# First folded weights of u made ahead of retention's last norm, constants moved off the vector engine, and other groups in the order of fours

## The chip, the cores and the metric

The kernel runs on one core of one Trainium2 chip. The metric is the time of one execution on the device, in microseconds (us); lower is better. A core has a matrix engine (TensorE, PE in the profile, its weight loads PEld), a vector engine (VectorE, DVE), a scalar engine (ScalarE, ACT), a general engine (GpSimd, POOL) and a queue engine (SyncE, SP) that issues the loads. Each engine works through its own instructions in order; semaphores join them.

## The reference

Two layers over 256 tokens of width 2048, with a second stream of 256 context tokens, batch 1, all in float32. Cut to what matters:

```python
# layer 0 (even): one input projection, two paths, one output projection
qx, kx, vx, gax, ux, gbx = _split_even(hx @ w_in)      # the same for the context: k and v
ret_x = _retention(rope(qx), rope(kx), vx, ...)        # 8 heads, both directions,
                                                       # each head's output divided by its rms
y_a = merge(ret_x) * silu(gax)
y_b = einsum(real(fft2(ux over tokens and channels of a group)), fno_w) * silu(gbx)
x   = x + gate * (concat(y_a, y_b) @ w_out)
# layer 1 (odd)
bg, cg, xt, g = split(h @ w_in1, 4)                    # 4 x 4096 columns
x   = x + gate * ((bg * conv3(cg * xt) * silu(g)) @ w_out1)
return rmsnorm(x)
```

Before each layer there is a modulated rmsnorm whose shift, scale and gate come from a conditioning vector times `ada_w`.

## The kernel before, in words

**Products in two halves.** Every weight and activation is cut into a high part in the rounded format float32r and a low part, the rest. A product is high times high, high times low and low times high. `cut` makes a high part with a copy on ACT (line 94) and the rest with a subtraction on DVE (line 59). Cut weights live in `slot()`s: rings of six `whi` and six `wlo` tiles of 128 x 512.

**Loads.** `load_raw` (line 85) fetches a weight tile of 128 x 2048 (1 MB) on SP's queue into a ring of three `raw` buffers. `split_w` cuts it in four pieces.

**Groups.** `group_t` computes 256 columns of a projection, transposed, for all tokens: `nkt` tiles of weights, four pieces each, and in each piece four blocks j of 128 x 128 with two matmuls: H (the high weights against both parts of the activations, 512 columns) and L (the low weights against the high part, 256 columns). The order of the eight is one of three lists: LOW (L0 H0 L1 H1 ...), HIGH (H0 L0 H1 L1 ...) and FOURS (H0 H1 H2 H3 L0 L1 L2 L3). The argument `orders` gives the list for the first piece and for all others. `lr` adds the two halves of a result on ACT (line 198) and DVE (line 65).

**Order of the work.** After every second piece `group_t` calls `hook()`, which takes the next function of the list `stages`: other work of the layer is laid in between so. `bg()` takes a task from a list of 64 reductions over `adaT`. The compiler's scheduler then orders the instructions of each engine by its own model of readiness; the written order is its priority.

**Stages of layer 0.** First the modulation, then four pairs of heads (`pr` 0 to 3): keys, queries and values, two groups for the gate (`sga`), with a head's `scores`, `values` and `norm` as stages. `norm` of a head is a matmul with ones into `ss`, a root on ACT (line 206), a reciprocal on DVE (line 207) and a product; the last norm of the last head is `h1[2]()` after the two gate groups of pair 3. Then `split_act` makes `yA`. Here the tile pool `rp` of retention closes, and the pool `fp` of the Fourier path opens on the same memory: its first writes wait for the last uses of `rp`.

**Fourier path.** The transform over tokens is folded: `fold_x` makes sums and differences of token pairs in `hf` (DVE lines 65, 68 and `split_act`); the first four of its eight tiles are made during pair 3, the others inside the `steps`. The weights of u are folded too: `half.fold(kc)` loads `w0u` (one load for two kc), makes the sum and the difference of two 512-column blocks with `add` (line 65) and `dif` (line 68) into tiles `ef` of the pool `fp`, and cuts both. `half.step(kc)` multiplies: six matmuls into `pu` and two into `pd`, 16 steps in each of two halves `u0` and `u1`; at its end it makes the next fold. The `pd` matmuls hold the end tokens (token 0 and 128 of the fold): their left side is `sd`, a tile of 16 x 32 columns, zero but for two columns that `ends(e)` copies out of `hf[e]`. `e0`, `rest`, `zero`, `umf` and `zero4` are constants that DVE fills (lines 590 to 612).

Between the steps runs `gate_of(g)` for g 0 to 7, a `group_t` of two tiles of `w0g` each. The stages from `gate_of(0)` on are:

```python
stages += [None, None, None, steps(0), steps(1), steps(2), steps(3, 4), ...]
```

so that step 0 comes at the fourth hook, behind the last piece of `gate_of(0)`.

**Projections.** `project` computes the output of a layer in eight blocks of 256 columns: seven `group_t` of four tiles (128 matmuls) and a last block `group_d`. Block 1 has orders (HIGH, FOURS), block 2 (HIGH, LOW), all others LOW. It runs once for each layer. The odd layer has 16 blocks b of four `group_t` of two tiles (64 matmuls): `tcg`, `txt`, `tbg`, `tg`. In b 1 and 2 `tcg` has (HIGH, FOURS) and `txt` (HIGH, LOW); all others are LOW.

Of the kernel before, what the change touches and what calls it, by code (L numbers as in the profile page):

```python
# [24 lines left out]
P = 128  # L25
# [10 lines left out]
def body(tc, a, out):  # L36
    nc = tc.nc
    es = ExitStack()
    with es:
# [43 lines left out]
        def load_raw(src):  # L83
            raw = wp.tile([P, 2048], F32, tag="raw", name="raw")
            nc.sync.dma_start(raw[:], src)
            return raw

        def slot():
            return (wp.tile([P, 512], F32R, tag="whi", bufs=6, name="whi")[:],
                    wp.tile([P, 512], F32R, tag="wlo", bufs=6, name="wlo")[:])  # L90
# [37 lines left out]
        HIGH = "H0 L0 H1 L1 H2 L2 H3 L3".split()  # L128
        FOURS = "H0 H1 H2 H3 L0 L1 L2 L3".split()

        SETTLE, AFTER = (HIGH, FOURS), (HIGH, LOW)

        def group_t(wd, i0, nkt, streams, orders=(LOW, LOW)):

            ps = [psum("gT") for _ in streams]
            last = nkt * 8 - 1
            for kt in range(nkt):
                raw = load_raw(wd[i0 + kt])
                bg()
                for pc, (hi, lo) in enumerate(split_w(raw)):  # L140
                    todo = orders[kt + pc > 0]
                    seen = set()
                    for what, j in ((x[0], int(x[1])) for x in todo):
                        k2, m = j // 2, j % 2
                        kc, c0 = kt * 8 + pc * 2 + k2, j * 128
                        n = 512 if what == "H" else 256
                        w = (hi if what == "H" else lo)[:, c0:c0 + 128]
                        for t, st in zip(ps, streams):
                            mm(t[:, m, 0:n], w, st[kc // 2][:, kc % 2, 0:n], kc == 0 and j not in seen,
                               kc == last and j in seen)  # L150
                        seen.add(j)
                    if pc % 2:
                        hook()
            return ps
# [331 lines left out]
        for pr in range(4):  # L486
            mk = [masks(2 * pr), masks(2 * pr + 1)]
            vbox = []
            def keys():
                tk, tkc = group_t(w0, iw[0], 2, [hx, hc])  # L490
                iw[0] += 2
                return rope(lr(rp, tk)[:], "k", K_CK, K_SK), lr(rp, tkc, "kc", 1)

            def queries():
                tq, = group_t(w0, iw[0], 2, [hx])
                iw[0] += 2
                return rope(lr(rp, tq)[:], "q", K_CQ, K_SQ)
# [12 lines left out]
            def heads():  # L510
                return [retention(hh, mk[hh], q, k, kc, lambda: vbox[0]) for hh in range(2)]

            if pr == 0:
                kc = rp.tile([P, 2, 256], F32, tag="kc", bufs=1, name="kc")
                nc.scalar.copy(kc[:], pk[:, 1, :].rearrange("p (m t) -> p m t", m=2))
                k = rope(pk[:, 0, :].rearrange("p (m t) -> p m t", m=2), "k", K_CK, K_SK)
                q = rope(pq[:].rearrange("p (m t) -> p m t", m=2), "q", K_CQ, K_SQ)
                h0, h1 = heads()
                stages += [None, h0[0], h1[0], h0[1], h0[2], h1[1], None, h1[2]]
                keep((pvx, pvc))  # L520
            elif pr < 3:
                k, kc = keys()
                q = queries()
                h0, h1 = heads()
                stages += [None, h0[0], None, h1[0], None, None, None, None]
                stages += [None, h0[1], None, h0[2], None, h1[1], None, h1[2]]
                keep(values())
            else:
                k, kc = keys()
                stages += [None, lambda: fold_x(rp, 0), None, None, None, lambda: fold_x(rp, 1), None, None]  # L530
                keep(values())
                stages += [None, lambda: fold_x(rp, 2), None, lambda: fold_x(rp, 3)]
                quiet[0] = True
                q = queries()
                h0, h1 = heads()
                stages += [h0[0], None, h0[1], h1[0], h0[2], None, h1[1], None]
            sga = []
            for hh in range(2):
                tg, = group_t(w0, iw[0], 2, [hx])
                iw[0] += 2  # L540
                sga.append(silu_lr(rp, tg, "sga"))
            if pr == 3:
                h1[2]()
            for hh, hd in enumerate((h0, h1)):
                y = yA[2 * pr + hh] = act_tile(YA[2 * pr + hh], f"yA{2 * pr + hh}")
                t = hd[3]["t"]
                mul(t[:], t[:], sga[hh][:])
                split_act(y, t[:])
# [38 lines left out]
            tab.update(dm=dm, dmh=dmh, dml=dml)  # L587

        e0 = fp.tile([P, 32], F32, name="e0")
        nc.vector.memset(e0[:], 0.0)  # L590
        nc.vector.memset(e0[:, 0:1], 1.0)
        rest = fp.tile([P, 1], F32, name="rest")
        nc.vector.memset(rest[:], 1.0)
        nc.vector.memset(rest[0:1, :], 0.0)
        sd = fp.tile([P, 16, 32], F32R, name="sd")
        zero = fp.tile([P, 512], F32, tag="t2", bufs=4, name="zero")
        nc.vector.memset(zero[:], 0.0)
        nc.vector.tensor_copy(sd[:], zero[:].rearrange("p (k c) -> p k c", k=16))

        def ends(e):  # L600
            nc.vector.tensor_copy(sd[:, 2 * e:2 * e + 2, 0:1], hf[e][:, :, 128:129].bitcast(F32))
            nc.vector.tensor_copy(sd[:, 2 * e:2 * e + 2, 1:2], hf[e][:, :, 384:385].bitcast(F32))

        for e in range(4):
            ends(e)
        umf = fp.tile([P, 16], F32, name="umf")
        nc.vector.memset(umf[:], 0.0)
        umh = fp.tile([P, 16], F32R, name="umh")
        uml = fp.tile([P, 16], F32R, name="uml")

        zero4 = fp.tile([P, 4], F32, name="zero4")
        nc.vector.memset(zero4[:], 0.0)

        ys = yA + [None] * 8

# [26 lines left out]
        class half:  # L642


            def __init__(self, hf):
                self.hf, self.pu = hf, None

            def fold(self, kc):

                if kc % 2 == 0:  # L650
                    self.raw = load_raw(a["w0u"][self.hf * 8 + kc // 2])
                r = self.raw[:].rearrange("p (k s c) -> p k s c", k=2, s=2)[:, kc % 2, :, :]
                self.w = []
                for op in (add, dif):
                    x = fp.tile([P, 512], F32, tag="ef", bufs=2, name="ef")
                    op(x[:], r[:, 0, :], r[:, 1, :])
                    self.w.append(slot())
                    cut(x[:], *self.w[-1])

            def step(self, kc):  # L660
                if self.pu is None:
                    self.pu, self.pd = psum("pu"), bank("pd")
                    self.fold(0)
                k2, w = kc % 2, self.w
                x = hf[kc // 2]
                for s in range(2):
# [122 lines left out]
        def steps(*kcs):  # L789
            def f():  # L790
                for kc in kcs:
                    u0.step(kc)
                    folds(kc)()
            return f

        stages += [None, None, None, steps(0), steps(1), steps(2), steps(3, 4), steps(5), steps(6), steps(7, 8), steps(9),
                   steps(10), steps(11, 12), both(steps(13), setup_tables), both(steps(14), setup_middle), both(steps(15), gs[0][0])]
        for g in range(4):
            gate_of(g)
# [27 lines left out]
        def project(wd, xs, gcol, xin, acc, first=None, post=None):  # L827
# [7 lines left out]
            for b in range(8):  # L835
                src = xin(b)
                quiet[0] = b >= 7 - (post is not None)
                if b < 7:
                    t = first if b == 0 and first is not None else group_t(wd, 4 * b, 4, [xs], *({1: (SETTLE,), 2: (AFTER,)}.get(b, ())))[0]
# [43 lines left out]
        w1 = a["w1"]  # L883
        y1 = []
        for b in range(16):
            tcg, = group_t(w1, b * 8, 2, [h1], *((SETTLE,) if b in (1, 2) else ()))
            scg = lr(l1, tcg, "scg", 2)
            txt, = group_t(w1, b * 8 + 2, 2, [h1], *((AFTER,) if b in (1, 2) else ()))
            z = lr(l1, txt, "z", 2)
            mul(z[:], z[:], scg[:])  # L890
            cv = l1.tile([P, 2, 256], F32, tag="cv", bufs=2, name="cv")
            for m in range(2):
# [5 lines left out]
                                               op0=ALU.mult, op1=ALU.add)  # L898
                nc.vector.scalar_tensor_tensor(c4[:, :, 0:63], z4[:, :, 1:64], w[2], c4[:, :, 0:63],
                                               op0=ALU.mult, op1=ALU.add)  # L900
            tbg, = group_t(w1, b * 8 + 4, 2, [h1])
            sbg = lr(l1, tbg)
            mul(cv[:], cv[:], sbg[:])
            tg, = group_t(w1, b * 8 + 6, 2, [h1])
            sg = silu_lr(l1, tg, "t2", 5)
            mul(cv[:], cv[:], sg[:])
            y1.append(act_tile(YA[b] if b < 8 else f"hx{b - 8}", f"y1_{b}"))
# [125 lines left out]
```

## Time and profile before

| | |
|---|---|
| median of three runs | 1823.37 us |
| lowest and highest of them | 1822.88 and 1826.58 us |
| the profiled execution, its own time | 1826.86 us |
| its span, mean granted clock | 1825.1 us, 0.988 |
| matmuls | 10086 |
| loads | 399.16 MB on SP's queue |

The span is the time from the first to the last instruction of the profiled execution; its own time has the start and the end beside it. In the rows below, an instruction is named by engine, line of the kernel, operation and tiles (output<-inputs); "L59 DVE ... wlo<-raw,whi" is the subtraction of a cut. "x" is a count. The time after the bar is the busy time in us and the mean of one in ns; what follows a second bar, or stands in square brackets, is idle time ahead of it and what ended it. The chain of work that ended last is followed back from the last instruction, at each step to what released it. The granted clock is the share of full speed at which PE ran.

### The profile page before, as it was taken

Reading aid. Unit: us, or ns where it says so; the run is one execution under the profiler, and the core shown is the slowest. Engines: PE = TensorE matmul, PEld = TensorE weight load, DVE = VectorE, ACT = ScalarE, POOL = GpSimd, SP = SyncE. Lnnn points to the kernel's source line nnn. Section 1 sums busy time; section 2 is a strip of 40 time slices with the busy share of each in tenths; the row PEclk is TensorE's granted clock in tenths of the full one; section 3 lists DMA queues with packets and bytes.
Section 4 is the critical chain, followed back from the end, with each engine's and each line's share of the span. In section 5 each row is a group of like instructions: output and inputs, shape, how many; then the busy total and the mean of one; then the engine's idle time right before and its main releaser. Section 6 shows DMA issues by size and latency. Waiting matters only on the chain.

```text
span 1825.1 us, 25950 instructions
## 1 busy us (share of the span) xinstructions
PE 1777.8 (97%) x10086; PEld 1514.6 (83%) x10086; DVE 1248.0 (68%) x2001; ACT 901.9 (49%) x1493; POOL 0.2 (0%) x4
## 2 busy tenths in 40 slices
PE   5999999999989999999999999999999999999997
PEld 3667888888877888888978888888888888888887
DVE  5348858758469788777677888666666666665554
ACT  4225626345455455444555555555555555555553
POOL 0000000000000000000000000000000000000000
PEclk9999999999989899999999999999999999999999
DMA  9886656655435556577647777555555555555552
GB/s 388 341 315 259 233 212 221 240 207 208 166 117 217 199 188 216 194 295 295 231 155 264 296 277 281 197 191 185 187 196 195 185 185 191 197 189 185 187 193 105
DMA packets 58732, 400.82 MB, mean 220 GB/s; under 512 B 6512, under 2 KB 6896, under 8 KB 11376
## 3 DMA queue, kind: packets, MB, share of 16 engines
q1 hardware_dynamic: 58608, 399.16, 59.8%
q8 instruction: 79, 1.29, 0.3%
q14 instruction: 45, 0.37, 0.1%
HBM read 397.03 MB, written 2.10 MB: 219 GB/s over the span
## 4 chain that ended last, share of the span: by engine, by line
PE 94%; DVE 3%; DMA 1%; ACT 1%; issue 0%; SPq 0%; DVEq 0%; ACTq 0%
PE gT L56 71%; PE gN L56 7%; PE gD L56 3%; PE pu L56 2%; PE gemv L56 2%; PE o L56 2%; PE pk L56 1%; PE pvx L56 1%; PE pvc L56 1%; PE pd L56 1%; DMA raw<-ada 1%; PE S L56 1%; PE pq L56 1%; DVE wlo L59 1%; PE pP L56 1%; PE py L56 0%
## 5 line engine op out<-in xcount | busy, mean ns | idle before, releaser
L94 ACT CAST whi<-raw 128x512 fp32r<-128x512 f32 x1024 | 628.3, 620 | 627.3 <-PE gT L56 469.4
L59 DVE TENSOR_TENSOR wlo<-raw,whi 128x512 fp32r<-128x512 f32 x1024 | 693.2, 688 | 344.4 <-ACT whi L94 334.5
L56 PE MATMUL gT<-h,whi 128*128 128x512 f32 x2048 | 707.6, 394 | 0.7 <-DVE h L215 0.7
L56 PE MATMUL gT<-h,wlo 128*128 128x256 f32 x2048 | 560.8, 278 | 3.4 <-ACT h L214 3.4
L56 PEld LDWEIGHTS gT<-h,whi 128*128 128x128 f32 x2048 | 383.3, 188 | 89.0 <-DVE h L215 1.2
L56 PEld LDWEIGHTS gT<-h,wlo 128*128 128x128 f32 x2048 | 383.4, 188 | 5.6 <-ACT h L214 3.8
L56 PE MATMUL gT<-hx,whi 128*128 128x512 f32 x576 | 209.4, 398 | 0.0
L388 DVE CUSTOM_DVE_ANT_0 raw<-raw,scb 128x2048 f32<-128x2048 f32 x64 | 146.5, 2290 | 54.0 <-DMA raw<-adaT 50.8
L56 PE MATMUL gT<-hx,wlo 128*128 128x256 f32 x576 | 165.2, 287 | 2.8 <-ACT v L507 1.6
L56 PE MATMUL gT<-y,whi 128*128 128x512 f32 x448 | 150.9, 394 | 0.0
L56 PEld LDWEIGHTS gT<-hx,whi 128*128 128x128 f32 x576 | 108.8, 189 | 21.3
L56 PEld LDWEIGHTS gT<-hx,wlo 128*128 128x128 f32 x576 | 109.5, 190 | 10.0 <-DVE wlo L59 2.7
L56 PE MATMUL gT<-y,wlo 128*128 128x256 f32 x448 | 116.9, 278 | 0.0
L56 PEld LDWEIGHTS gT<-y,whi 128*128 128x128 f32 x448 | 82.9, 188 | 18.2
L198 ACT COPY lr_r<-gT 128x512 f32<-128x512 f32 x103 | 60.5, 587 | 65.7 <-PE gT L56 65.4
L56 PEld LDWEIGHTS gT<-y,wlo 128*128 128x128 f32 x448 | 82.1, 188 | 1.4
L56 PE MATMUL gT<-yA,whi 128*128 128x512 f32 x224 | 77.5, 398 | 0.0
L56 PE MATMUL gT<-yB,whi 128*128 128x512 f32 x224 | 76.9, 398 | 0.0
L65 DVE TENSOR_TENSOR t<-gT,lr_r 128x512 f32<-128x512 f32 x68 | 46.9, 689 | 29.9 <-ACT lr_r L198 29.7
L56 PE MATMUL gT<-yA,wlo 128*128 128x256 f32 x224 | 59.9, 281 | 0.6 <-DVE wlo L59 0.6
L56 PE MATMUL gN<-whi,hx 128*128 128x512 f32 x192 | 59.7, 392 | 0.0
L56 PE MATMUL gN<-whi,hc 128*128 128x512 f32 x192 | 59.7, 391 | 0.0
(283 smaller groups left out, 2162.0 us busy)
## 6 DMA issues: line engine op xcount, KB each, us to landing
raw<-w SPq DMA_DIRECT2D x168, 1024.0 KB, 4.8
raw<-adaT SPq DMA_DIRECT2D x64, 1024.0 KB, 4.9
raw<-ada SPq DMA_DIRECT2D x32, 1024.0 KB, 7.1
raw<-w0o SPq DMA_DIRECT2D x32, 1024.0 KB, 4.8
raw<-w1o SPq DMA_DIRECT2D x32, 1024.0 KB, 4.8
raw<-w0g SPq DMA_DIRECT2D x16, 1024.0 KB, 4.8
raw<-w0u SPq DMA_DIRECT2D x16, 1024.0 KB, 4.9
raw<-w0s SPq DMA_DIRECT2D x8, 1024.0 KB, 5.6
```

Of the source, the lines that this page charges most:

```text
L56: nc.tensor.matmul(o, l, r, start=start, stop=stop, skip_group_check=True)
L59: nc.vector.tensor_tensor(o, x, hi.bitcast(F32), op=ALU.subtract)
L65: nc.vector.tensor_tensor(o, x, y, op=ALU.add)
L94: nc.scalar.copy(hi, x)
L198: nc.scalar.copy(r[:], t[:, :, 256:512])
L388: nc.vector.tensor_tensor_reduce(out=raw[:], in0=raw[:], in1=scb[:], scale=1.0, scalar=0.0, op0=ALU.mult, op1=ALU.add, accum_out=gv[:, j:j ...
```

## The change

1. **First folds.** In pair 3, ahead of `h1[2]()`, the first tile of `w0u` is loaded and its four folds (kc 0 and 1, `add` and `dif`) are made into two tiles `first_u`, which lie in the memory of `hc[6]` and `hc[7]`, free by then. `fold(0)` and `fold(1)` of `u0` then only cut. `u0.fold(0)` becomes a stage of its own, one hook ahead of step 0.
2. **Constants and end tokens.** The fills of `e0`, `rest`, `zero`, `umf` and `zero4` go from DVE to GpSimd. The copy of zeros into `sd` and the copies of the end tokens go to ACT, one copy for the two columns where there were two.
3. **Fours.** `orders` is a list that the pieces take in turn. SETTLE is HIGH and seven FOURS, AFTER is HIGH and seven LOW: eight pieces, a group of two tiles. In `project`, blocks 3 and 4 have SETTLE + AFTER, block 1 and 2 nothing. In the odd layer `tbg` of b 0 and 1 has SETTLE and `tg` of b 0 and 1 AFTER, beside `tcg` and `txt` of b 1 and 2 as before.

```diff
-        SETTLE, AFTER = (HIGH, FOURS), (HIGH, LOW)
+        SETTLE, AFTER = [HIGH] + [FOURS] * 7, [HIGH] + [LOW] * 7
-        def group_t(wd, i0, nkt, streams, orders=(LOW, LOW)):
+        def group_t(wd, i0, nkt, streams, orders=(LOW,)):
...
-                    todo = orders[kt + pc > 0]
+                    todo = orders[(kt * 4 + pc) % len(orders)]
...
             if pr == 3:
+                raw = load_raw(a["w0u"][0])[:].rearrange("p (k s c) -> p k s c", k=2, s=2)
+                first_u = [acts.tile([P, 2, 512], F32, tag=HF[6 + k2], name="first_u") for k2 in range(2)]
+                for k2 in range(2):
+                    for i, op in enumerate((add, dif)):
+                        op(first_u[k2][:, i, :], raw[:, k2, 0, :], raw[:, k2, 1, :])
                 h1[2]()
...
-        nc.vector.memset(e0[:], 0.0)
-        nc.vector.memset(e0[:, 0:1], 1.0)
+        nc.gpsimd.memset(e0[:], 0.0)
+        nc.gpsimd.memset(e0[:, 0:1], 1.0)
...
-        nc.vector.memset(zero[:], 0.0)
-        nc.vector.tensor_copy(sd[:], zero[:].rearrange("p (k c) -> p k c", k=16))
+        nc.gpsimd.memset(zero[:], 0.0)
+        nc.scalar.copy(sd[:], zero[:].rearrange("p (k c) -> p k c", k=16))
         def ends(e):
-            nc.vector.tensor_copy(sd[:, 2 * e:2 * e + 2, 0:1], hf[e][:, :, 128:129].bitcast(F32))
-            nc.vector.tensor_copy(sd[:, 2 * e:2 * e + 2, 1:2], hf[e][:, :, 384:385].bitcast(F32))
+            nc.scalar.copy(sd[:, 2 * e:2 * e + 2, 0:2], hf[e][:, :, 128:512:256].bitcast(F32))
...
             def fold(self, kc):
+                self.w = []
+                if self.hf == 0 and kc < 2:
+                    for i in range(2):
+                        self.w.append(slot())
+                        cut(first_u[kc][:, i, :], *self.w[-1])
+                    return
...
-        stages += [None, None, None, steps(0), ...
+        stages += [None, None, lambda: u0.fold(0), steps(0), ...
...
-                    t = ... group_t(wd, 4 * b, 4, [xs], *({1: (SETTLE,), 2: (AFTER,)}.get(b, ())))[0]
+                    t = ... group_t(wd, 4 * b, 4, [xs], SETTLE + AFTER if b in (3, 4) else (LOW,))[0]
...
-            tbg, = group_t(w1, b * 8 + 4, 2, [h1])
+            tbg, = group_t(w1, b * 8 + 4, 2, [h1], SETTLE if b in (0, 1) else (LOW,))
...
-            tg, = group_t(w1, b * 8 + 6, 2, [h1])
+            tg, = group_t(w1, b * 8 + 6, 2, [h1], AFTER if b in (0, 1) else (LOW,))
```

More of the change, by code (lines that the diff above doesn't have):

```diff
@@ L589, in body @@
         e0 = fp.tile([P, 32], F32, name="e0")
-        nc.vector.memset(e0[:], 0.0)
-        nc.vector.memset(e0[:, 0:1], 1.0)
+        nc.gpsimd.memset(e0[:], 0.0)
+        nc.gpsimd.memset(e0[:, 0:1], 1.0)
         rest = fp.tile([P, 1], F32, name="rest")
-        nc.vector.memset(rest[:], 1.0)
-        nc.vector.memset(rest[0:1, :], 0.0)
+        nc.gpsimd.memset(rest[:], 1.0)
+        nc.gpsimd.memset(rest[0:1, :], 0.0)
         sd = fp.tile([P, 16, 32], F32R, name="sd")
         zero = fp.tile([P, 512], F32, tag="t2", bufs=4, name="zero")
-        nc.vector.memset(zero[:], 0.0)
-        nc.vector.tensor_copy(sd[:], zero[:].rearrange("p (k c) -> p k c", k=16))
+        nc.gpsimd.memset(zero[:], 0.0)
+        nc.scalar.copy(sd[:], zero[:].rearrange("p (k c) -> p k c", k=16))
         def ends(e):
-            nc.vector.tensor_copy(sd[:, 2 * e:2 * e + 2, 0:1], hf[e][:, :, 128:129].bitcast(F32))
-            nc.vector.tensor_copy(sd[:, 2 * e:2 * e + 2, 1:2], hf[e][:, :, 384:385].bitcast(F32))
+            nc.scalar.copy(sd[:, 2 * e:2 * e + 2, 0:2], hf[e][:, :, 128:512:256].bitcast(F32))
         for e in range(4):
@@ L606, in body @@
         umf = fp.tile([P, 16], F32, name="umf")
-        nc.vector.memset(umf[:], 0.0)
+        nc.gpsimd.memset(umf[:], 0.0)
         umh = fp.tile([P, 16], F32R, name="umh")
@@ L611, in body @@
         zero4 = fp.tile([P, 4], F32, name="zero4")
-        nc.vector.memset(zero4[:], 0.0)
+        nc.gpsimd.memset(zero4[:], 0.0)
         ys = yA + [None] * 8
@@ L645, in __init__ @@
             def __init__(self, hf):
-                self.hf, self.pu = hf, None
+                self.hf, self.pu, self.w = hf, None, None
             def fold(self, kc):
+                self.w = []
[4 more added lines that the diff above has]
+                    return
                 if kc % 2 == 0:
@@ L652, in fold @@
                 r = self.raw[:].rearrange("p (k s c) -> p k s c", k=2, s=2)[:, kc % 2, :, :]
-                self.w = []
                 for op in (add, dif):
@@ L662, in step @@
                     self.pu, self.pd = psum("pu"), bank("pd")
-                    self.fold(0)
+                    if self.w is None:
+                        self.fold(0)
                 k2, w = kc % 2, self.w
@@ L794, in steps @@
             return f
-        stages += [None, None, None, steps(0), steps(1), steps(2), steps(3, 4), steps(5), steps(6), steps(7, 8), steps(9),
+        stages += [None, None, lambda: u0.fold(0), steps(0), steps(1), steps(2), steps(3, 4), steps(5), steps(6), steps(7, 8), steps(9),
                    steps(10), steps(11, 12), both(steps(13), setup_tables), both(steps(14), setup_middle), both(steps(15), gs[0][0])]
@@ L838, in project @@
                 if b < 7:
-                    t = first if b == 0 and first is not None else group_t(wd, 4 * b, 4, [xs], *({1: (SETTLE,), 2: (AFTER,)}.get(b, ())))[0]
+                    t = first if b == 0 and first is not None else group_t(wd, 4 * b, 4, [xs], SETTLE + AFTER if b in (3, 4) else (LOW,))[0]
                     s = lr(l1, t)
@@ L885, in body @@
         for b in range(16):
-            tcg, = group_t(w1, b * 8, 2, [h1], *((SETTLE,) if b in (1, 2) else ()))
+            tcg, = group_t(w1, b * 8, 2, [h1], SETTLE if b in (1, 2) else (LOW,))
             scg = lr(l1, tcg, "scg", 2)
-            txt, = group_t(w1, b * 8 + 2, 2, [h1], *((AFTER,) if b in (1, 2) else ()))
+            txt, = group_t(w1, b * 8 + 2, 2, [h1], AFTER if b in (1, 2) else (LOW,))
             z = lr(l1, txt, "z", 2)
```

## The prediction

> **What bounds the kernel now.** I read the page first (busy times and the chain that ended last), then that chain around the one stretch where another engine than PE carries it, then the windows there, then PE's pace in the long stages.
>
> ```profile
> PE 1777.8 (97%) x10086; PEld 1514.6 (83%) x10086; DVE 1248.0 (68%) x2001; ACT 901.9 (49%) x1493; POOL 0.2 (0%) x4
> ...
> PE 94%; DVE 3%; DMA 1%; ACT 1%; issue 0%; SPq 0%; DVEq 0%; ACTq 0%
> ```
>
> PE is the bound: 94% of the chain. So time can come only from places where PE waits or is slow. The chain behind the last norm of retention, up to the second gate's first pieces, start and length in us:
>
> ```profile
> 536.02 0.09 DVE e L590
> 536.18 0.48 DVE zero L597
> 536.67 0.07 DVE ef L65
> 536.75 0.52 issue
> 537.27 0.69 DVE ef L68
> 537.96 0.60 DVE hs L65
> 538.56 0.34 DVE sd L598
> 538.90 0.60 DVE wlo L59
> ...
> 541.41 0.07 DVE sd L602
> 541.48 0.59 DVE ef L65
> 542.07 0.60 DVE t L65
> 542.67 0.60 DVE ef L68
> ...
> 547.81 6.05 PE gT L56 x24
> ```
>
> From 536.0 to 547.8 the chain is DVE's: constants, folds, end tokens, subtractions. PE meanwhile (columns: window, length, then busy time and count of PE, PEld, DVE, ACT, POOL, then granted clock):
>
> ```profile
> 500.00:508.20 8.20, 8.20 (x44) 7.22 (x43) 2.62 (x4) 1.84 (x4) 0.00 (x0) 1.00 0.34 128
> 528.10:531.30 3.20, 3.20 (x21) 2.81 (x20) 0.03 (x2) 2.91 (x4) 0.00 (x0) 1.00 0.64 207
> 534.29:537.71 3.42, 0.51 (x3) 0.19 (x1) 2.53 (x11) 0.88 (x2) 0.00 (x0) 1.00 0.22 58
> 537.71:551.36 13.65, 11.84 (x27) 6.99 (x28) 13.65 (x39) 8.68 (x15) 0.00 (x0) 0.50 0.27 88
> 551.40:575.00 23.60, 23.60 (x122) 19.11 (x122) 23.00 (x49) 12.58 (x23) 0.00 (x0) 1.00 0.53 197
> 155.40:158.80 3.40, 1.76 (x10) 1.29 (x9) 3.32 (x4) 3.36 (x6) 0.00 (x0) 1.00 0.74 311
> ```
>
> On the timeline, PE's last matmul before the gap, and ACT's first instruction after the root:
>
> ```profile
> 534.41 0.39 PE L56 MATMUL gT<-hx,whi 128*128 128x512 f32 x1
> ```
>
> ```profile
> 534.53 0.62 ACT L220 CAST yA<-ot 128x512 fp32r<-128x512 f32 x1 [3.27 <-DVE ot L62]
> ```
>
> PE stops at 534.80. After a window with 0.51 us of PE work the clock falls to 0.50 for 13.65 us. DVE has no pause there (13.65 of 13.65) and almost none up to 575 (23.00 of 23.60).
>
> **PE's pace** is the second place. The same matmuls run at two paces; matmuls on gT in two windows, then two pieces in the order of fours on the timeline:
>
> ```profile
> 781.00:890.00 109.00, 109.00 (x619) 94.49 (x618) 2.77 (x4) 2.35 (x4) 1.00 0.76 286
> 1025.00:1655.00 630.00, 630.00 (x3636) 550.96 (x3635) 38.04 (x55) 32.40 (x55) 1.00 0.57 206
> ```
>
> ```profile
> 975.47 0.63 PE L56 MATMUL gT<-h,wlo 128*128 128x256 f32 x4
> 975.94 1.09 PE L56 MATMUL gT<-h,whi 128*128 128x512 f32 x4
> 976.87 0.64 PE L56 MATMUL gT<-h,wlo 128*128 128x256 f32 x4
> ```
>
> 109.00/619 = 176.1 ns a matmul in the first output projection (slow rhythm), 630.00/3636 = 173.3 in the odd layer (quick rhythm), at the same full clock. A piece of fours, eight matmuls, takes 976.87 - 975.47 = 1.40 us, 175 each; a matmul of 512 columns is (976.87 - 975.94) / 4 = 0.233 us. Before, the fours of block 1 of the first projection left the slow rhythm behind them; those of the odd layer and of the second projection left the quick one.
>
> **The change part by part.**
>
> *First folds moved.* Four DVE operations (add and dif for kc 0 and 1) leave the chain: kc 0 from 536.67 to 537.96, 1.3 us; kc 1 0.59 + 0.60 = 1.2 us. Ahead of the norm the same four cost 4 x 0.60 = 2.4 us of DVE, put at nothing: in 500.0 to 508.2 DVE has 5.6 us idle, and 3.2 idle in the window at 528.1, where it waits for the root. If that cover were gone the norm would start later by up to 2.4. They issue one load, which moves ahead of the gate's two (issues on SP's queue, the page's median to landing, and a wait of DVE for such a load):
>
> ```profile
> 494.83 5.47 SPq L85 DMA_DIRECT2D raw<-w0g  x2
> 512.65 0.33 SPq L85 DMA_DIRECT2D raw<-w0u  x1
> ```
>
> ```profile
> raw<-w0u SPq DMA_DIRECT2D x16, 1024.0 KB, 4.9
> ```
>
> ```profile
> 580.99 0.69 DVE L65 TENSOR_TENSOR ef<-raw 128x512 f32<-128x512 f32 x1 [0.85 <-DMA raw<-w0u]
> ```
>
> w0u then starts near 494.8, the gate's second load near 512.65 instead of about 500 and lands near 517.6. Six weight slots of 1.4 us lie between a cut and its use, and PE reaches that load's pieces four pieces before 534.80, at 529.2: nothing. The ring gains, since w0u's buffer was held from 512.65 until the fold at 543.
>
> The cuts of kc 0 and 1 no longer wait for fold tiles that stand on retention's memory. ACT, idle for 3.27 us before 534.53, can make them; one or two of the four subtractions (0.60 each) fit on DVE in the window at 528.1 or during ACT's 0.62 at 534.53, when DVE waits for it. I take 1.5 of them, 0.9 us; ends 0.6 and 1.2 (more if all four fit).
>
> *Constants to GpSimd, sd to ACT.* Off the chain on DVE: memsets 536.02 to 536.66 (with zero's 0.48), 0.64; the cast of sd 0.34; sixteen end-token casts at 0.07, 1.1. What replaces them, by the nearest rows (timeline of POOL, a group of the page, timeline of ACT):
>
> ```profile
> 0.24 0.10 POOL L1025 MEMSET const-float32-0.0<- 128x1 f32 x1 [0.24 <-issue]
> ```
>
> ```profile
> L94 ACT CAST whi<-raw 128x512 fp32r<-128x512 f32 x1024 | 628.3, 620 | 627.3 <-PE gT L56 469.4
> ```
>
> ```profile
> 632.17 0.17 ACT L637 COPY umf<-pm 128x8 f32<-128x8 f32 x1 [7.34 <-PE pm L56]
> ```
>
> The trace has no GpSimd fill of 512 columns. Ends: 0.48 as on DVE, and 0.8, DVE's 0.48 scaled by 0.10 over 0.06 for the one-column fills; later still is a rival. I take 0.8, the row being GpSimd's own. Then: retention's memory free at 536.0, four small fills 4 x 0.10, zeros 0.8, ACT's copy 0.62, four end copies 4 x 0.17: sd ready near 538.4, against 541.4 now. ACT has room (8.68 busy of 13.65). Behind ACT's copy queue the next cuts, up to 1.3 us late, with PE's first step already supplied; behind the later end copies, which wait for DVE's half of hf, cuts queue too, each by less than the 0.60 of that half. The pd matmuls wait for sd, and PE stands in order behind them.
>
> *What PE gains.* Ceiling: between 534.80 and 551.40 PE did 12 pu and 4 pd matmuls (16 x 0.233 = 3.7 us) and 12 gT (12 x 0.173 = 2.1): 5.8 of 16.6 us, so at most 10.8 can be had. With pu of kc 0 starting at 534.8 and pd at 538.4, no window is as empty as the one with 0.51 us; 1.76 us in one kept the clock at 1.00 at 155.4. So I expect no half clock. Floor: DVE, full until 575, is late next. Sum of what leaves it: 0.64 + 1.3 + 1.2 + 0.34 + 1.1 + 0.9 = 5.5 us. The gate's pieces cannot be cut sooner than that, so I take **5.5**, not 10.8.
>
> *Fours.* An expression of 16 entries taken in turn is, for a group of two tiles, one HIGH and seven FOURS, as before. First projection: fours move from block 1 to 3 and 4, half a block each. A block is 128 x 0.176 = 22.5 us and the last begins at
>
> ```profile
> 891.21 22.93 PE gD L56 x191
> ```
>
> so block 3 starts near 801 and its fours end near 812. From there 79 us, 448 matmuls, can run 2.8 ns quicker: 1.25, less 56 matmuls of fours in block 4 at 1.7 ns more, 0.1. Odd layer: the quick rhythm starts one group of 64 earlier, +0.2, and one more group of fours costs 0.1. Second projection: 112 matmuls in fours for 120, nothing. Sum **1.2**; ends 0 (the rhythm stays) and 1.9.
>
> **Sum.** 5.5 + 1.2 = 6.7. The profiled execution takes 1826.86 (span 1825.1): 1820.2 after. The median of the three runs shown is 1823.37, 3.5 less; no row shows what sets them apart, so I subtract the same: **1816.7**. A measurement tells about 0.2%, 3.65 us, from no change.
>
> **Rivals.**
>
> *A. PE refills the gap.* If DVE's backlog is mostly work wanted later (fold_x of tiles 4 to 7), PE gets its ceiling: 10.8 + 1.2, 1811.4. For it: fold_x stands in that backlog. Against: the gate's pieces queue behind the same operations.
>
> *B. The zeros come late and ACT and PE stand behind them.* If sd is ready no sooner than at 541.4, PE does step 0 (1.4 us) and stops for 5 us; the clock halves again, and in ten half-clock microseconds it does 5.0 of work: 6.4 against 5.8. Gain 0.6 + 1.2: 1821.6. For it: DVE runs two-input subtractions without a pause from 536, and the only GpSimd fills seen, at 0.24, ran beside nothing. Against: even 2 us for the fill leaves sd before 540. It decides from a fill of some 3.8 us. The Trainium skill speaks for this way in GPSIMD Engine Reference, 1. Specifications: GpSimd's SBUF interfaces contend with DVE instructions of two SBUF inputs. By that rule the time is 1821.6. The skill's SBUF — State Buffer, Who interferes with whom, narrows it to a GpSimd instruction that reads SBUF, which a fill does not; by that, 1816.7. No run here shows either.
>
> *C. Loads bind next.* DVE waited 0.85 us for w0u at 580.99. If that landing cannot move, the 5.5 is given back there and 1.2 is left: 1822.2. Against: the load is issued when DVE frees a buffer, and moves with it.
>
> *D. The slow rhythm after the odd layer's last fours (slower than before).* The trace shows one exit of that kind, at 779. If the fours of block 2 leave it, 3636 matmuls take 2.8 ns more, 10.2 us, against the gain of 5.5 + 1.2: 1826.9. It decides at that one group: from 6.7 us lost there the change is no gain. Against: two exits with the same count of fours there left the quick one.
>
> **How the numbers follow.** Forecast 0.57, A 0.14, B 0.15, C 0.08, D 0.06. Range: down to A's side, 1811.2, and up to B, 1821.7; it leaves out C, D and a little of A, under 0.2. The likeliest alone: 1814.5 to 1819, from DVE's ends (4.6 with no subtraction placed, 7.0 with all four) and the rhythm's 0 to 1.9. Faster by over 0.2%: the forecast, A and the better part of B's doubt, 0.73; same: B and C, 0.21; slower: D, 0.06.
>
> **What would show it.** Right: four folds on first_u before 531; pu at 534.8 to 535.5; pd near 538.5; no half clock there, or a shorter one; DVE still full from 536 on and the first gate piece near 542; after the first projection's block 3 or 4, 173.3 ns a matmul. Wrong: a fill on POOL of 3.8 us or more, the chain there through POOL or ACT, DVE waiting on raw more than 2 us before 600, or 176 ns in 1025 to 1655.

## The result, and the profile after

The changed kernel takes 1835.62 us (median of 4 runs, 1834.88 to 1838.19), the kernel before beside it 1823.12 (4 runs, 1822.84 to 1826.58): a ratio of 1.0067 with a 95% interval of 1.0049 to 1.0084. It is slower by 12.5 us where 6.7 us less was forecast.

The profiled execution of the changed kernel took 1834.88 us, its span 1833.0; before, 1826.86 and 1825.1. So the two traces differ by 7.9 us, less than the medians, because the profiled execution of before was 3.7 us above its median and that of after 0.7 below. The page of the changed kernel, busy time by engine and the chain's shares:

```profile
PE 1787.0 (97%) x10086; PEld 1517.3 (83%) x10086; DVE 1246.2 (68%) x1977; ACT 903.8 (49%) x1502; POOL 1.0 (0%) x11
...
PE 94%; DVE 3%; DMA 1%; ACT 1%; issue 1%; SPq 0%; DVEq 0%; ACTq 0%
```

The same 10086 matmuls keep PE busy 9.2 us longer (1787.0 against 1777.8). Where that is, three marks tell that stand in the chain of every kernel here: the stretch of 114 gT matmuls ahead of the transition, the last block gD of the first projection, the last block of the second. The chain of the changed kernel (start, length):

```profile
479.21 20.14 PE gT L56 x114
...
884.71 22.93 PE gD L56 x191
...
1797.05 23.04 PE gD L56 x192
```

The same chain of the kernel before, whose middle mark (891.21) stands in the prediction:

```profile
478.78 20.14 PE gT L56 x114
...
1789.14 23.03 PE gD L56 x192
```

From the first mark to the second: 891.21 - 478.78 = 412.43 us before, 405.50 after, so 6.9 less. From the second to the third: 897.93 before, 912.34 after, so 14.4 more. With 0.4 at the start the sum is the 7.9 of the spans. The transition gained what was forecast and somewhat more; the odd layer, which the change hardly touches, lost twice that.

**The transition after.** Windows of the changed kernel, the same as those of before, then the one half-clock stretch left between 500 and 900 us (busy time and count of PE, PEld, DVE, ACT, POOL, then granted clock):

```profile
500.00:508.20 8.20, 8.20 (x46) 7.22 (x46) 6.83 (x11) 2.51 (x4) 0.00 (x0) 1.00 0.62 226
...
534.29:537.71 3.42, 3.42 (x18) 2.83 (x17) 2.75 (x3) 2.28 (x5) 0.00 (x0) 1.00 0.00 0
537.71:551.36 13.65, 11.36 (x55) 7.80 (x53) 13.52 (x29) 9.96 (x21) 0.78 (x7) 1.00 0.49 168
551.40:575.00 23.60, 21.56 (x104) 16.14 (x105) 23.27 (x45) 12.67 (x26) 0.00 (x0) 1.00 0.52 184
...
623.57:630.40 6.83, 6.83 (x28) 6.21 (x28) 0.74 (x2) 1.03 (x4) 0.00 (x0) 0.50 0.17 70
```

PE has no empty window (3.42 of 3.42 where it had 0.51), the clock stays at 1.00, and in the 13.65 us after it PE does 55 matmuls instead of 27. DVE is as full as before. On the timeline, cut to some lines: on DVE the first of the four moved folds, the last two of their four cuts, the norm's reciprocal and the next fold; on PE the first pu, the first gate piece, the first pd and PE's first wait for DVE behind it; on GpSimd the fill of zeros, and on ACT the copies of the end tokens:

```profile
500.13 0.69 DVE L65 TENSOR_TENSOR first_u<-raw 128x512 f32<-128x512 f32 x1 [1.12 <-DMA raw<-w0u]
...
532.65 1.29 DVE L59 TENSOR_TENSOR wlo<-first_u,whi 128x512 fp32r<-128x512 f32 x2 [1.68 <-ACT whi L94]
534.96 1.75 DVE L207 RECIPROCAL rstd<-rstd 128x256 f32<-128x256 f32 x1 [1.01 <-ACT rstd L206]
...
541.07 0.69 DVE L65 TENSOR_TENSOR ef<-raw 128x512 f32<-128x512 f32 x1
```

```profile
535.07 0.63 PE L56 MATMUL pu<-whi,hf 128*128 128x512 f32 x2
...
537.83 0.28 PE L56 MATMUL gT<-hx,wlo 128*128 128x256 f32 x1
...
543.93 0.39 PE L56 MATMUL pd<-whi,sd 128*32 128x512 f32 x1
...
548.74 0.50 PE L56 MATMUL pu<-wlo,hf 128*128 128x512 f32 x1 [1.33 <-DVE wlo L59]
```

```profile
541.24 0.53 POOL L603 MEMSET zero<- 128x512 f32 x1
```

```profile
543.37 0.49 ACT L607 CAST sd<-hf 128x4 fp32r<-128x4 f32 x4
```

**PE's pace after.** Matmuls on gT in the changed kernel: behind the fours of block 4 of the first projection, then the odd layer in the window that was shown of before, then the odd layer and the second projection up to its last block:

```profile
829.40:884.30 54.90, 54.90 (x313) 47.61 (x312) 1.38 (x2) 1.17 (x2) 1.00 0.72 268
...
1025.00:1655.00 630.00, 630.00 (x3567) 546.33 (x3567) 38.04 (x55) 32.28 (x55) 1.00 0.56 203
935.00:1797.00 862.00, 862.00 (x4883) 747.91 (x4882) 48.38 (x70) 41.05 (x70) 1.00 0.57 206
```

and the kernel before from where it became quick to its end:

```profile
980.00:1789.00 809.00, 809.00 (x4666) 707.35 (x4664) 45.60 (x66) 38.43 (x66) 1.00 0.58 209
```

In the window 1025 to 1655 PE does 3567 matmuls where it did 3636, at the same full clock and 630.00 us busy: 176.6 ns each, the slow rhythm. The whole stretch is at 862.00/4883 = 176.5 ns; before, 809.00/4666 = 173.4. 4666 times the difference of 3.1 is 14.5 us, all that was lost. Busy time alone does not show this: PE is at 100% in both.

### The profile page after: what moved, and what is told of

It is laid out like the page before. It is cut to its first block, busy times and chain, and to the rows that moved or that the text cites. A ratio compares the mean times of both kernels' runs of the same rounds, so it can differ in the third digit from the quotient of the medians.

```text
span 1833.0 us, 25969 instructions
## 1 busy us (share of the span) xinstructions
PE 1787.0 (97%) x10086; PEld 1517.3 (83%) x10086; DVE 1246.2 (68%) x1977; ACT 903.8 (49%) x1502; POOL 1.0 (0%) x11
## 4 chain that ended last, share of the span: by engine, by line
PE 94%; DVE 3%; DMA 1%; ACT 1%; issue 1%; SPq 0%; DVEq 0%; ACTq 0%
PE gT L56 71%; PE gN L56 7%; PE gD L56 3%; PE pu L56 2%; PE gemv L56 2%; PE o L56 2%; PE pk L56 1%; PE pvx L56 1%; PE pvc L56 1%; DVE wlo L59 1%; DMA raw<-ada 1%; PE pd L56 1%; PE S L56 1%; PE pq L56 1%; PE pP L56 1%
## 5 line engine op out<-in xcount | busy, mean ns | idle before, releaser
L56 PE MATMUL gT<-h,whi 128*128 128x512 f32 x2048 | 715.3, 399 | 0.3 <-DVE h L215 0.3
L56 PE MATMUL gT<-yB,wlo 128*128 128x256 f32 x224 | 62.4, 281 | 0.0
```

Source lines behind the costliest of these rows:

```text
L56: nc.tensor.matmul(o, l, r, start=start, stop=stop, skip_group_check=True)
```

## The experiments

**Reading the rhythm.** The start-to-start times of single matmuls, from the traces, tell more than means. In alternating order (LOW or HIGH, the same but where they join) the slow rhythm is a cycle of three pairs, the quick one of two. H stands for a matmul with the high weights, L for one with the low, the number for the ns since the start of the one before:

```
slow   H113 L233 H117 L241 H120 L236   three pairs, 1060 ns: 353.3 a pair
quick  H113 L232 H118 L231             two pairs, 694 ns: 347 a pair (346.7 over long stretches)
fours  X: L232 L118 L119 L118 H117 H235 H233 H236   pieces alternate X, Y, X, Y
       Y: L224 L117 L120 L120 H120 H234 H236 H228   out of X quick, out of Y slow
```

(A line of fours shows the four L of one piece and the four H of the next.) So where PE stands in its pattern when the order changes back decides what follows for the next thousands of matmuls. Two theories stood at the start. P: each piece of fours takes PE from one of two patterns to the other, so that the count of pieces decides. Q: the rhythm follows from something else in the changed program.

**The parts apart.** `old_fours` is the changed kernel with parts 1 and 2 and the old orders; `new_fours` the kernel before with part 3 alone; `six_last` the changed kernel with one piece of fours fewer at the last place.

```diff
# six_last, against the changed kernel
-            tcg, = group_t(w1, b * 8, 2, [h1], SETTLE if b in (1, 2) else (LOW,))
+            tcg, = group_t(w1, b * 8, 2, [h1], [HIGH] + [FOURS] * 6 + [HIGH] if b == 2 else SETTLE if b == 1 else (LOW,))
```

> The changed kernel with the fours where they were before (parts 1 and 2 of the change alone). Theory P: a run of pieces in the order of fours keeps or turns PE's rhythm by its count and by how many pieces in the order HIGH stand ahead of it; in the kernel before, the scheduler had itself turned the last piece ahead of the first fours of the odd layer into HIGH, so that 8 pairs stood ahead of them instead of 4, and that turned the slow rhythm into the quick one. This kernel has that extra HIGH piece too, so: quick (173.3 ns a matmul) from block 1 of the odd layer on, and the gain of layer 0 shows alone: 1816 to 1818 us, 5 to 7 below the kernel before. Rival Q: parts 1 and 2 (other tiles, other order on PE) bring the slow pace with them: 176 ns in the odd layer, about 1829 to 1836 us.

> The kernel before with the new places of the fours alone (part 3). Theory P: no extra HIGH piece stands ahead of the fours, all their counts are 7, so the slow rhythm in which the odd layer begins is kept at every one: 176.6 ns a matmul through both projections and the odd layer, 12 to 15 us over the kernel before, 1835 to 1840 us. Rival Q (the slow pace comes with parts 1 and 2): no more than 1 us from the kernel before, 1822 to 1825 us.

> The changed kernel with six instead of seven pieces of fours in one group only, tcg of block 2 of the odd layer (its eighth piece is in the order HIGH). Theory P (the rhythm changes at each piece of fours, so an even count turns what an odd count keeps): slow up to there, quick from about 1018 us of the span to the end: 688 us of it shorter by 1.9%, 13 us, and the second projection shorter by 1 to 2: 1820 to 1823 us. Rival Q (the pace belongs to the kernel's tiles or to the edits in layer 0): unchanged, 1834 to 1837. Rival R (fours simply cost time, the fewer the better): 0.1 us less, 1835.

Beside 1824.03 for the kernel before, `old_fours` took 1835.17 (ratio 1.0065, 1.0052 to 1.0078), `new_fours` 1839.96 (1.0090, 1.0077 to 1.0102), `six_last` 1819.52 (0.9980, 0.9971 to 0.9988). The same window of each, in this order:

```profile
1025.00:1655.00 630.00, 630.00 (x3567) 546.30 (x3566) 38.03 (x55) 32.28 (x55) 1.00 0.56 203
```

```profile
1025.00:1655.00 630.00, 630.00 (x3569) 546.33 (x3568) 38.71 (x56) 32.87 (x56) 1.00 0.57 204
```

```profile
1025.00:1655.00 630.00, 630.00 (x3637) 550.97 (x3636) 38.72 (x56) 32.98 (x56) 1.00 0.57 206
```

One piece of eight matmuls in another order takes 16 us off the whole: P holds for `six_last` (0.5 us under its range), which has parts 1 and 2 and is quick, so that Q falls; R, 0.1 us for a piece, falls with it. Part 3 alone makes the kernel before slow, against Q again. But `old_fours` missed, and its time is in the range that Q gave: it has the old orders and was slow all the same. The pieces of the odd layer, read off the order of PE's instructions, explain half of it. In the kernel before the compiler's scheduler had itself turned the last piece ahead of the first fours from LOW to HIGH, so that two HIGH pieces, seven FOURS and one HIGH stood in a row. That, not the count of seven, turned slow into quick at 980 us; the other two exits were then found quick and left so. `old_fours` has the same word of pieces and stays slow. The start-to-start times where the two HIGH pieces begin (the bar stands ahead of the second of two H in a row):

```
before     ... L241 H120 L236 H113 | H232 L236 H116 L224 H118 L233 H118 L240 H120 ...   slow into the fours, quick out of them
old_fours  ... H120 L236 H113 L233 H117 | H241 L238 H116 L230 H117 L230 H117 ...        quick at once, slow out of the fours
```

What differs is the place in the cycle of three pairs at which the word begins: behind L236 H113 in the one, behind L233 H117 in the other.

**Is it the place in the cycle?** `two_high_12` and `two_high_13` are `old_fours` with the same word (two HIGH, seven FOURS, one HIGH) put in again, behind 12 or 13 LOW pieces from the third group of block 1 on. The fours of block 2 make way for it, and one HIGH piece more in each projection came in with it, on which more below. Cut to the word:

```diff
# two_high_12, against the changed kernel (two_high_13: six FOURS, one LOW in tcg; five LOW, one FOURS in tg)
-            tcg, = group_t(w1, b * 8, 2, [h1], SETTLE if b in (1, 2) else (LOW,))
+            tcg, = group_t(w1, b * 8, 2, [h1], {1: SETTLE, 2: [FOURS] * 5 + [HIGH] * 1 + [LOW] * 2}.get(b, (LOW,)))
...
-            tg, = group_t(w1, b * 8 + 6, 2, [h1], AFTER if b in (0, 1) else (LOW,))
+            tg, = group_t(w1, b * 8 + 6, 2, [h1], [LOW] * 4 + [HIGH] * 2 + [FOURS] * 2 if b == 1 else (LOW,))
```

> The kernel with parts 1 and 2 on the old orders came out slow although the same pieces (two of the order high-first, seven of fours, one of high-first) turned the kernel before to the quick pairs of 346.7 ns. Theory P2: what a word of pieces does depends on which of the three pairs of the slow cycle it meets; in the kernel before, the gap at the second high-first matmul in a row was 232 ns, in that slow one 241. So the same word is put in again one piece (four pairs, that is one place further in a cycle of three pairs) at a time. Here two pieces high-first, seven of fours and one high-first start after 12 pieces of low-first counted from the third group of block 1 of the odd layer. P2, going step by step through the gaps that the traces show, gives at the junction the gap 232 that the kernel before had, and quick pairs (346.7) from there to the end: 1818 to 1822 us. Rival R (a piece's place in the cycle has no say; parity of the pieces alone): as the other of this pair, both slow, 1832 to 1838, or both quick. Rival C (chance decides at each entry): either.

> The same word one piece later, after 13 pieces of low-first. P2: at the junction another of the three gaps (236 or 241), the two high-first pieces turn the pairs quick for a moment, seven of fours turn them back, and the pairs stay at 353.3 ns to the end: 1832 to 1838 us. R: as two_high_12. C: either.

They took 1820.49 and 1830.43 us (one run each, before 1823.27), and the windows are:

```profile
1025.00:1655.00 630.00, 630.00 (x3635) 550.65 (x3633) 38.72 (x56) 32.97 (x56) 1.00 0.57 207
```

```profile
1025.00:1655.00 630.00, 630.00 (x3567) 546.34 (x3567) 38.05 (x55) 32.27 (x55) 1.00 0.56 203
```

The second H in a row came 233 ns after the first in the one and 241 in the other, as forecast, and the one is quick, the other slow. R falls. Chance alone (C) would have to have hit at all eight places where the traces have this word: quick at four of 232 or 233, slow at four of 241 (the last section names the kernels). The 1830.43 is 1.6 under the range given: both kernels also had a lone HIGH piece in each projection (an order list of eight pieces runs twice through a group of sixteen), and in `two_high_13` each of the two turned 353 ns a pair into 347. In `two_high_12` the first did the same, while the second, which met quick pairs, turned them slow. That suggested a simpler rule than fours.

**Shorter, or even?** `five_last` is `six_last` with `[HIGH] + [FOURS] * 5 + [HIGH] * 2` at the last place.

> six_last with five pieces of fours in the last place instead of six, and two high-first pieces behind them instead of one; all else as in six_last (1819.5 us) and the changed kernel (1835.6). P2 (the count's parity decides): an odd count, so the pairs stay at 353.3 ns, 1833 to 1838 us. Rival S (seven is too long, any shorter run of fours settles): quick pairs from 1019 us, 1818 to 1822. The second high-first piece behind is the one thing that P2 has seen in no trace in this place.

1834.20 us, and

```profile
1025.00:1655.00 630.00, 630.00 (x3568) 546.31 (x3567) 38.04 (x55) 32.28 (x55) 1.00 0.57 202
```

Five is slow like seven, six is quick: the parity decides, not the length. That is for places met at 232 or 233, as all the even counts here are.

**No fours at all, and one HIGH piece.** `all_low` has every piece of the changed kernel LOW. `one_high` has one HIGH piece at two places and no fours. `six_once` has the six fours at two places and keeps the sevens of block 0 of the odd layer.

```diff
# one_high, against the changed kernel
-    ... group_t(wd, 4 * b, 4, [xs], SETTLE + AFTER if b in (3, 4) else (LOW,))
+    ... group_t(wd, 4 * b, 4, [xs], [HIGH] + [LOW] * 15 if b == 3 and gcol == 0 else (LOW,))
-    txt, = group_t(w1, b * 8 + 2, 2, [h1], AFTER if b in (1, 2) else (LOW,))
+    txt, = group_t(w1, b * 8 + 2, 2, [h1], AFTER if b == 1 else (LOW,))       # HIGH, seven LOW; all other groups (LOW,)
# six_once
+    ... group_t(wd, 4 * b, 4, [xs], [HIGH] + [FOURS] * 6 + [HIGH] + AFTER if b == 3 and gcol == 0 else (LOW,))
+    tcg, = group_t(w1, b * 8, 2, [h1], [HIGH] + [FOURS] * 6 + [HIGH] if b == 1 else (LOW,))
```

> The changed kernel with every piece in the order low-first: parts 1 and 2 whole, no fours and no high-first pieces at all. P2: seven fours behind one high-first piece only keep the rhythm that they find, so without them nothing changes: pairs of 353.3 ns in the first projection and in the odd layer to the end, 1833 to 1838 us, as the changed kernel. Rival F (the fours of the change do turn something, and it is turned back later): another time by over 2 us. Rival E (the pieces' own stalls would leave the quick rhythm if no order were changed): 1817 to 1822 us.

> The changed kernel with no piece of fours at all, and one single piece in the order high-first (then low-first again) at two places: ahead of block 3 of the first projection and ahead of the second group of block 1 of the odd layer. Theory P2 in its simplest form, from what two_high_12 and two_high_13 showed by the way (a lone high-first piece in the first projection ended pairs of 353 ns, one in the second projection ended pairs of 347 ns): one high-first piece among low-first ones turns the rhythm over, whichever it was, and an even count of fours after it turns it too, an odd one turns it back. So here the pairs go to 346.7 ns at about 797 us and again at about 975 us, and stay there: six_last's 1819.5 less 88 x 1.9% = 1.6 in the first projection and 44 x 1.9% = 0.8 in the odd layer, 1816.5 to 1818 us, ratio 0.996. Rival F (it is the fours that turn the rhythm, the high-first piece only leads in): slow all through, 1833 to 1838 us. Rival C (it hangs on the place in the slow cycle met): one of the two places, or neither.

> The changed kernel with six pieces of fours in place of seven, a high-first piece ahead and behind, once in the first projection (block 3) and once in the odd layer (first group of block 1), and the other places of the change taken out, save the sevens of block 0's third group, which keep what they find. P2: quick pairs from about 811 us and again from about 974 us to the end: 1819.5 - 1.4 - 0.85 = 1817.3, 1816.5 to 1818 us. Rival C: quick at one of the two places only, 1818 to 1820 or 1833 to 1836.

Beside 1824.41 for the kernel before: `all_low` 1834.69 (1.0054, 1.0041 to 1.0067), `one_high` 1817.95 (0.9968, 0.9957 to 0.9980), `six_once` 1819.76 (0.9970, 0.9957 to 0.9982). Without any fours the time is within 1 us of the changed kernel's: its groups of sevens, four in the odd layer and two in each projection, do nothing at all: each finds the slow rhythm and leaves it. `all_low`, in the window:

```profile
1025.00:1655.00 630.00, 630.00 (x3567) 546.31 (x3567) 38.06 (x55) 32.28 (x55) 1.00 0.56 203
```

`one_high`, ahead of and behind each of its two HIGH pieces:

```profile
764.00:793.00 29.00, 29.00 (x166) 25.13 (x165) 1.38 (x2) 1.18 (x2) 1.00 0.83 310
797.00:881.00 84.00, 84.00 (x486) 73.44 (x486) 2.08 (x3) 1.77 (x3) 1.00 0.77 285
935.00:970.00 35.00, 35.00 (x200) 30.35 (x199) 2.08 (x3) 1.76 (x3) 1.00 0.62 219
972.00:1779.00 807.00, 807.00 (x4658) 705.44 (x4657) 44.97 (x65) 38.29 (x65) 1.00 0.58 209
```

29.00/166 and 35.00/200 are 174.7 and 175.0 with the windows' edges (176.6 from start to start); 84.00/486 is 172.8 and 807.00/4658 173.2. One piece of eight matmuls, in an order that differs from its neighbours' only where they join, turns the rhythm for the 4658 that follow. Its two places met the cycle at 232 and at 241, and both turned. F falls, and so does C, by which at most one would have turned. `six_once` does the same by fours (3637 in the window 1025 to 1655, as `six_last`); its median is 1.8 above the range expected, though its profiled run took 1817.20. Its trace shows quick pairs from both places on, so the miss is not in the rhythm. `one_high` is the fastest version found; it beats the kernel before by 6.5 us and `all_low`, which stands for the changed one and ran on the same chip, by 16.7.

**Parts 1 and 2 apart.** `folds_only` and `consts_only` are the kernel before with one of them.

> Part 1 alone on the kernel before: the first folded weights of u made ahead of the last norm of retention; constants, ends and orders as before. The mark is the end of the last gT matmul of the first projection: 890.8 us in the trace of before, 884.3 in that of the kernel with all three parts, and 884.8 with parts 1 and 2 on the old orders. Theory W (VectorE work sets the transition, so what each part takes from VectorE there adds up): by the prediction's own terms part 1 is 1.3+1.2+0.9 = 3.4 us of 5.5 and, scaled to the 6.5 seen, 4.0: the mark at 886.4 to 887.4, and the other part alone makes up the rest. Rival V (one part alone opens the gap: the half clock at 537 us goes as soon as the folds are early, and the constants were never last): 884 to 885.5. Rival U (the constants alone carry it): 890 to 891. The half clock at 537: gone by W and V. The total depends on which rhythm the odd layer is left in and says nothing on this: about 1817 to 1821 with the quick pairs, 1829 to 1839 with the slow ones.

> Part 2 alone on the kernel before: the zeros by GpSimd, the row of end tokens by ScalarE with half as many copies; folds and orders as before. Same mark, 890.8 us before and 884.3 with all. Theory W: by the prediction's terms part 2 is 0.64+0.34+1.1 = 2.1 us of 5.5, scaled 2.5: the mark at 888.0 to 889.0. Rival V: 890 to 891 (nothing without the early folds). Rival U: 884 to 885.5. The half clock at 537 us stays by V, and may stay by W, since the folds still wait for the subtractions. The total again depends on the odd layer's rhythm: 1819 to 1823 quick, 1831 to 1841 slow.

The two marks of the transition, `folds_only`, then `consts_only`, then `old_fours` with both:

```profile
477.89 20.14 PE gT L56 x114
...
886.73 22.93 PE gD L56 x191
```

```profile
476.51 20.14 PE gT L56 x114
...
884.34 22.93 PE gD L56 x191
```

```profile
478.22 20.14 PE gT L56 x114
...
885.16 22.93 PE gD L56 x191
```

From mark to mark 408.84, 407.83 and 406.94 us against 412.43: gains of 3.6, 4.6 and 5.5. The expectations went by the second mark alone, which moves with the start of a run (the first mark lies between 476.5 and 479.2); by it alone `consts_only` would have come near U's range. With the difference the folds are worth what W gave them at the unscaled 3.4, the constants twice their 2.1, and V and U fall. W's sum falls too: 3.6 + 4.6 is not 5.5. `folds_only` has step 0 in the gap at 534 and the full clock until 551, then 3.41 us of half; `consts_only` still has the half clock from 534.7, for 10.24 us instead of 13.65, and the later one at 623 for 6.83 instead of 10.24. `old_fours` has that later one at 10.24, as before. So some 1.7 of the 4.6 is of the later stretch (an estimate: half of the 3.41 us less of half clock), which comes at either length in kernels with the same transition. Without it the constants bring 2.9, near W's scaled 2.5, and the two parts 6.5 where both together bring 5.5. The last 1.0 was not taken apart, and each of the two kernels was traced once. Both kernels came out quick in the odd layer (1822.44 and 1820.05 us, one run each): the word of two HIGH and seven FOURS met the cycle at 232 and at 233 there.

## Why the prediction was wrong

**The step that failed is "Fours".** It gave part 3 a gain of 1.2 with "ends 0 (the rhythm stays) and 1.9". In the odd layer the rhythm did not stay as it was: 176.6 ns a matmul from 1025 to 1655, the prediction's own sign of being wrong, and 14.4 us lost from the second mark to the third. In the first projection, where 1.25 was to come, it stayed slow: 54.90/313 = 175.4 ns a matmul with the window's edges, 353.2 a pair from start to start. The sum closes in the traces: forecast -6.7, measured +8.0 between the two profiled executions; the difference of 14.7 is, within 0.1, 14.4 lost in the odd layer and after, 1.2 of fours that did not come, 0.4 of the start, less 1.4 by which the transition gained more.

The row for that step was there and I misread it. "Two exits with the same count of fours there left the quick one" was true, but I took what stood behind the fours for what the fours do. A count of seven leaves what it finds. The exits of the kernel before were quick because the first of them was entered through two HIGH pieces at the right place in the cycle, and one of these was put there by the scheduler, in no line of the source. The start-to-start times ahead of and behind the fours, which the trace of before has, show it; the prediction used means over windows.

**Rival D happened, at 0.06.** Its place was right (the odd layer is left slow), its price was not: 10.2 for the 3636 matmuls of one window, where 4666 run to the end of the second projection, 14.4 to 14.7. It also put the cause in the last fours "leaving" the slow rhythm; they found it. And its chance was set by how many exits had been quick, which were not independent: three exits in a chain, of which the first made the quick rhythm and the two behind it kept what they found.

**The transition was right in size.** Step by step: four folds on first_u before 531 (500.13 to 503.2); pu at 534.8 to 535.5 (535.07); no half clock there; DVE full from 536 on (13.52 of 13.65, 23.27 of 23.60). The fill of zeros took 0.53 us, at the lower of the ends 0.48 and 0.8, so 0.8 was too much. Of the four subtractions I placed 1.5 ahead; all four went there (the last two at 532.65), which is the upper end. Wrong: pd near 538.5 came at 543.93, and the first gate piece "near 542" at 537.83. The norm's reciprocal is at 534.96, 3.7 us later than before, where the prediction put the work ahead of the norm at nothing and at most 2.4. So retention's memory is free only at 541, and the constants with it: `sd`, said to be ready near 538.4, is so at 543.86 (543.37 + 0.49), later than the 541.4 of before. PE had no wait up to 547 all the same, since it had gate pieces to do between, 32 matmuls from 537.83 to 543.47, where the prediction said that these cannot be cut sooner. So 5.5 was right in size (5.5 in `old_fours`, 6.9 in the changed kernel) by terms that are off in both directions, and that they come out so near is in part luck. Between traces of kernels with the same transition and a slow first projection it is 5.4 to 7.0; the larger ones have the later half-clock stretch, shown above for the changed kernel, at 6.83 us, the others at 10.24, as before.

**Rivals A, B and C.** A's ceiling of 10.8 was not reached: DVE's subtractions are late next, as said (PE waits 1.33 for one at 548.74). B needed a fill of 3.8 us. It ran at 541.24 beside a DVE addition of two SBUF inputs that began at 541.07; that addition took 0.69 like its neighbours, and the fill 0.53. That is as the Trainium skill has it in SBUF — State Buffer, Who interferes with whom (only a GpSimd instruction that reads SBUF contends with such an addition), and not by the wider rule of GPSIMD Engine Reference, 1. Specifications. C: DVE's longest wait for w0u between 500 and 620 is 1.2 us, under the 2 that would have told against the forecast.

**The base.** The prediction subtracted 3.5 us from the profiled execution to come to the median and did the same for the changed kernel. That execution of before was high (1826.86 against 1823.12), the changed kernel's was not (1834.88 against 1835.62), so 4.2 us of the 18.9 by which the median missed are of this kind (3.5 and 0.7), and 14.7 are those told above. On one chip the medians give 15.65 for the rhythm (`old_fours` less `six_last`) and 4.5 to 4.8 for the transition (before less `six_last`, `new_fours` less `old_fours`).

## What to carry to other kernels

Two loops with the same matmuls, the same clock and PE 100% busy can differ by 2%: look at start-to-start times of single instructions on both sides of a place where the order changes, not only at means, and ask whether what stands behind it was made there or only passed on. When a trick works in a trace, take it out once before building on it: `all_low` against the changed kernel would have shown that seven fours are nothing, and one piece turned over does what the fours were there for. And read the order as the scheduler left it, not as the source has it.

## What the runs showed of the hardware that was not expected

PE has two stable rhythms for the same alternating stream of 512- and 256-column float32r matmuls, each with its own weights: 346.7 ns a pair in a cycle of two pairs, and 353.3 in a cycle of three. (The quick pairs also come in a cycle of one, L230 H117, in short stretches: 24 matmuls in a row up to 928 us of before.) Neither decays: 4882 matmuls in a row kept the slow one (`all_low`), 4663 the quick one (`one_high`). A single piece with the two kinds exchanged, so that two H and later two L stand next to each other, turned slow into quick in five places of three kernels (the H came at 232 and at 241 in `one_high`) and quick into slow in the one place where it met quick pairs. An even count of fours behind a HIGH piece turned it in `six_last` and `six_once`, met at 232 or 233, odd ones (five, seven, and fifteen in the second projection of the old orders) did not; two HIGH pieces with seven fours turned it at 232 to 233 (`before`, `folds_only`, `consts_only`, the second such word of `two_high_12`) and not at 241 (`old_fours`, the first word of `two_high_12`, both of `two_high_13`). No piece written HIGH met the third place of the cycle, 236. Not every exchange turns it: where the scheduler itself exchanged four matmuls at the start of the odd layer (at 935.18 us of before, met at 233), slow stayed slow.

The Trainium skill, TensorE: Matmul & The Clock Gate, Wait — 56ns, not 53.3ns?, gives warm matmuls N / 2.4 GHz plus about 2.5 ns start to start; for a pair of 512 and 256 columns that is an estimate of 325 ns by that page. The traces have 346.7 and 353.3, so the measurement decides here: a pair takes 22 or 28 ns more than that estimate. What inside PE holds the state (the 256-column matmuls come at 224 to 241 behind an H and at 113 to 120 behind an L) was not settled; no run here varied the weight loads.

Half-clock stretches also come and go in this transition. `six_once` had, in its profiled run, two of 3.41 us at 550 and 564, and `two_high_13` one at 561, that the changed kernel did not have, with the same work there. Executions of one kernel differ by 2 to 7 us, and such stretches may be part of it, which no run here tested. The first of those of `six_once` in its windows:

```profile
550.29:553.70 3.41, 3.41 (x11) 2.92 (x12) 3.41 (x9) 1.01 (x3) 0.00 (x0) 0.50 0.05 19
```
